# Splitting the first four convolutions of the up projection into an early and a late part

## The chip, the cores and the metric

The kernel runs on one core of a Trainium2 chip. The metric is the device time of one execution in microseconds (us). The core has five engines that run side by side and meet only through semaphores: TensorE (PE, matmuls into PSUM), VectorE (DVE), ScalarE (ACT), GpSimd (POOL) and SyncE (SP), which here only issues transfers. PSUM, the memory that TensorE writes, has eight banks of 128 x 512 float32 values.

## The reference

One layer of a hybrid block on x of 256 rows and 2048 columns: three kinds of attention, a gate, an output projection, then a feed-forward part. Only the feed-forward part matters here:

```python
h2 = rms_norm(x, g_ffn[l])
u = causal_depthwise_conv(h2 @ w_up[l], conv_w[l], conv_b[l])   # 3 taps along the rows
u_gate, u_val = jnp.split(u, 2, axis=-1)                        # 5632 columns each
x = x + (jax.nn.silu(u_gate) * u_val) @ w_down[l]
```

All arithmetic is float32.

## The kernel before, in words

A float32 product is made of cheaper ones: each weight tile `raw` is split into a high half `hi` (a cast on ACT, L141) and a low half `lo` (raw minus hi, a subtraction on DVE, L142), and TensorE multiplies both. `piece` (L135 to L146) is one such step: SP loads 128 x 1024 values, ACT casts, DVE subtracts. There are four buffers each for raw, hi and lo, so ACT can cast a piece only when TensorE has finished with the piece four before it, and SP can load a piece only when the low half of the piece four before it is made.

The up stage goes over `w_up` in groups of four column tiles of 128 (the loop over `f0`), for the gate half (s = 0) and the value half (s = 1) of each. A group is eight pieces (k = 0, 2, ..., 14); each piece is eight pairs of matmuls: L1148 (hi, 512 wide) and L1149 (lo, 256 wide). A group fills four PSUM banks, and the next group the other four. Its names are `u_0`, `hi_u_0_6`, `lo_u_1_8` and so on: the first number is s, the second k. The third group is called `u_0` again (f0 = 4, s = 0). Here "first group" is f0 = 0, s = 0, "second" is f0 = 0, s = 1, "third" is f0 = 4, s = 0.

After a group four convolutions follow, one per bank (`conv`, L1109 to L1132). Each empties its bank (ACT copies one half to `cr`, L1114; DVE adds the other, L1116), multiplies by `rbc` on DVE (L1117, into a padded tile `u`), applies tap 2 and the bias on ACT (L1120), the two other taps on DVE (L1121, L1122), and then either a Silu on ACT (s = 0, L1124) or, for s = 1, the product with the gate half and a split into halves for the next stage (L1128, L175, L176).

`rbc` is the reciprocal root of the mean square of each row of x, laid along the free dimension and repeated on all partitions. It isn't there when the up stage starts: the first group of matmuls runs on rows that aren't normalised yet, and the sums of squares come in meanwhile. When they are done (L551 to L534 in the trace), POOL stores 256 numbers to DRAM (L1044, `rstd_row`) and loads them back to all partitions (L1045, `rbc`).

The order: convolutions are generators that `later` queues; `tick`, called after each piece, advances at most two of them (WINDOW) by one step. Instructions are then put by a scheduler into one fixed order per engine, which each engine follows strictly; `in_order` (`keep_in_program_order`) pins an instruction to its place in the program among the pinned ones. Beside all this `weight_sums` adds up parts of the later stage's weights (`pre_d`, DVE L267 to L269), with loads on SP's queue (L258).

Of the kernel before, what the change touches and what calls it, by code (L numbers as in the profile page):

```python
# [9 lines left out]
F32 = mybir.dt.float32  # L10
F32R = mybir.dt.float32r
AF = mybir.ActivationFunctionType
ALU = mybir.AluOpType
AX = mybir.AxisListType

P = 128
S = 256
# [24 lines left out]
def hybrid_block(  # L42
# [25 lines left out]
    nc = tc.nc  # L68
# [12 lines left out]
    def bank(name):  # L81
        return pp.tile([P, 512], F32, tag="bank", name=name)
# [14 lines left out]
    def later(gen):  # L97
        waiting.append(gen)
# [3 lines left out]
    def tick(beside=True):  # L102
        if beside:
            for g in background:
                next(g, None)
        while waiting and len(active) < WINDOW:
            active.append([waiting.popleft(), 0])
        for a in list(active):
            if a[1] > 0:
                a[1] -= 1  # L110
                continue
            try:
                a[1] = next(a[0]) or 0
            except StopIteration:
                active.remove(a)
# [19 lines left out]
    def piece(src, a, n, name):  # L135
        raw = wp.tile([P, PIECE], F32, tag="raw", name=f"raw_{name}")
        hi = wp.tile([P, PIECE], F32R, tag="hi", bufs=SBUFS, name=f"hi_{name}")
        lo = wp.tile([P, PIECE], F32R, tag="lo", bufs=SBUFS, name=f"lo_{name}")
        m = a * n
        pin(nc.sync.dma_start(raw[:, :m].rearrange("p (a n) -> p a n", a=a), src))  # L140
        pin(nc.scalar.copy(hi[:, :m], raw[:, :m]))  # L141
        pin(nc.vector.tensor_tensor(lo[:, :m], raw[:, :m], hi[:, :m].bitcast(F32), ALU.subtract))  # L142
        return (
            hi[:, :m].rearrange("p (a n) -> p a n", a=a),
            lo[:, :m].rearrange("p (a n) -> p a n", a=a),
        )  # L146
# [9 lines left out]
    def product(x_of, w, nk, n0, n, name):  # L156

        ps = [bank(f"{name}_{t}") for t in range(NT)]
        wv = w.rearrange("(k p) n -> p k n", p=P)
        for k in range(0, nk, 2):  # L160
            a = min(2, nk - k)
            wh, wl = piece(wv[:, k : k + a, n0 : n0 + n], a, n, f"{name}_{k}")
            order = [(j, t) for j in range(a) for t in range(NT)]
            if k + a == nk:
                order.sort(key=lambda jt: jt[1])
            for j, t in order:
                xk = x_of(k + j)
                xs_ = xk[:, t * P : (t + 1) * P], xk[:, S + t * P : S + (t + 1) * P]
                three(ps[t][:, :n], *xs_, (wh[:, j], wl[:, j]), k + j == 0, k + j == nk - 1)
            tick()  # L170
        return ps

    def split_to(dst, src):

        nc.scalar.copy(dst[..., :S], src)  # L175
        nc.vector.tensor_tensor(dst[..., S:], src, dst[..., :S].bitcast(F32), ALU.subtract)  # L176
# [53 lines left out]
    in_order = tc.keep_in_program_order  # L230
# [343 lines left out]
    def plain_heads(ps, rs, name):  # L574
        y = rows_of(block(f"y_{name}"))
        for t in range(NT):
            nc.scalar.activation(y[:, t], ps[t], AF.Copy, scale=rs[:, t : t + 1])
        return y

    def norm_heads(ps, rs, name):  # L580

        y = plain_heads(ps, rs, name)
        ss = sm.tile([P, NT * 4], F32, tag="hss", name=f"hss_{name}")
        for t in range(NT):
            sq = junk(f"sq_{name}_{t}")
            nc.scalar.activation(sq, y[:, t], AF.Square)
            nc.vector.tensor_reduce(
                ss[:, t * 4 : (t + 1) * 4], sq.rearrange("p (h d) -> p h d", h=4), AX.X, ALU.add
            )
        r = sm.tile([P, NT * 4], F32, tag="hr", name=f"hr_{name}")  # L590
        rsqrt_mean(r, ss, NT * 4, HD, name)
        for t in range(NT):
            yt = y[:, t].rearrange("p (h d) -> p h d", h=4)
            nc.vector.tensor_tensor(
                yt, yt, r[:, t * 4 : (t + 1) * 4].unsqueeze(2).to_broadcast([P, 4, HD]), ALU.mult
            )
        return y
# [105 lines left out]
    y = norm_heads(kv[0], rstd_m, "mk")  # L703
# [26 lines left out]
    ps = proj(C_MQ, MEM_W, "mq")  # L730
# [5 lines left out]
    y = norm_heads(ps, rstd, "mq")  # L736
# [30 lines left out]
    for c in range(3):  # L767
        ps = proj(c * 512, 512, f"f{c}")
        qk[c] = heads_of(block(f"qk_fox{c}"))
        y = norm_heads(ps, rstd, f"f{c}")  # L770
# [5 lines left out]
    ps = proj(1536, 512, "f3")  # L776
# [3 lines left out]
    ps = proj(2048, 262, "f4")  # L780
# [74 lines left out]
    for c in range(3):  # L855
        ps = proj(C_SB + c * 512, 512, f"s{c}")
        qs[c] = heads_of(block(f"qk_sb{c}"))
        y = plain_heads(ps, rstd, f"s{c}")
# [49 lines left out]
    ps = proj(C_SB + 1536, 512, "s3")  # L908
# [4 lines left out]
    ps = proj(C_SB + 2048, 256, "s4")  # L913
# [39 lines left out]
    for m in range(2):  # L953
        gate = []
        for b, plan in enumerate(g_plans[m]):
# [40 lines left out]
            if not plan:  # L996
                biases()
                for n in range(2):
                    ps = proj(c0 + n * 512, 512, f"g{n}_{b}")
# [12 lines left out]
        for n in range(2):  # L1012
            acc = gate[branches[0][3]][n]
            for i, (w, k0, nk, b) in enumerate(branches):
                ps = product(lambda k: oT[:, k0 + k], w[0], nk, (2 * m + n) * 512, 512, f"b{2 * m + n}_{b}")
# [16 lines left out]
    rbc = cst.tile([P, S], F32, name="rbc")  # L1032
# [56 lines left out]
    def a_pair(p):  # L1089
        if p < FA // 2:  # L1090
            return aT[:, 2 * p : 2 * p + 2]
        if p not in ends:
            ends[p] = ff.tile([P, 2, 2 * S], F32R, tag=f"end{p - FA // 2}", bufs=1, name=f"end_{p}")
        return ends[p]

    uv = ctx.enter_context(ExitStack())
    cp = uv.enter_context(tc.tile_pool(name="cp", bufs=2))
    upv = w_up[0].rearrange("(k p) n -> p k n", p=P)
    pads = []

    def padded():
        for i in range(2):
            u = cp.tile([P, S + 2], F32, bufs=1, name=f"u_{i}")
            nc.vector.memset(u[:, 0:2], 0.0)
            pads.append(u)

    ys = {}

    def conv(ps, f, s):  # L1109
        if not pads:  # L1110
            padded()
        ct = s * FT + f
        cr = cp.tile([P, S], F32, tag="cr", bufs=2, name=f"cr_{f}_{s}")
        nc.scalar.copy(cr, ps[:, S:])  # L1114
        u = pads[f % 2]
        nc.vector.tensor_tensor(cr, cr, ps[:, :S], ALU.add)  # L1116
        nc.vector.tensor_tensor(u[:, 2:], cr, rbc, ALU.mult)  # L1117
        y = cp.tile([P, S], F32, tag="y", bufs=6, name=f"y_{f}_{s}")
        tap = lambda j: taps[:, j, ct : ct + 1]
        nc.scalar.activation(y, u[:, 2:], AF.Identity, scale=tap(2), bias=tap(3))  # L1120
        nc.vector.scalar_tensor_tensor(y, u[:, 1 : S + 1], tap(1), y, ALU.mult, ALU.add)  # L1121
        nc.vector.scalar_tensor_tensor(y, u[:, 0:S], tap(0), y, ALU.mult, ALU.add)  # L1122
        if s == 0:
            nc.scalar.activation(y, y, AF.Silu)  # L1124
            ys[f] = y
        else:
            g = ys.pop(f)
            nc.vector.tensor_tensor(g, g, y, ALU.mult)  # L1128
            split_to(a_pair(f // 2)[:, f % 2], g)
        return  # L1130
        yield

    for f0 in range(0, FT, 4):
        if f0 == FA:
            assert not halves
            for g in background:
                deque(g, 0)
            background.clear()
        for s in range(2):
            ps = [bank(f"u{f0 + i}_{s}") for i in range(4)]  # L1140
            c0 = s * D_FF + f0 * P
            for k in range(0, KT, 2):
                hi, lo = piece(upv[:, k : k + 2, c0 : c0 + 512], 2, 512, f"u{f0}_{s}_{k}")
                for j in range(2):
                    first, last = k + j == 0, k + j == KT - 1
                    for i in range(4):
                        c = slice(i * P, (i + 1) * P)
                        nc.tensor.matmul(ps[i], lhsT=hi[:, j, c], rhs=hT(k + j), start=first, stop=False)  # L1148
                        nc.tensor.matmul(  # L1149
                            ps[i][:, :S], lhsT=lo[:, j, c], rhs=hT(k + j)[:, :S], start=False, stop=last  # L1150
                        )
                tick()
            for i in range(4):
                later(conv(ps[i], f0 + i, s))

# [89 lines left out]
```

## Time and profile before

| | us |
|---|---|
| three runs: median (lowest to highest) | 1480.77 (1472.53 to 1480.96) |
| the profiled execution | 1473.09 |
| its span, first to last instruction | 1471.4 |
| PE busy | 1462.6 (99%) |
| DVE busy | 1192.1 (81%) |
| ACT busy | 838.9 (57%) |
| mean granted TensorE clock | 0.998 |

"Busy" of PE means that some matmul was in flight; a matmul that runs at a lower clock counts as busy for its longer time. An engine's line in a timeline gives the start, the duration, the line of the kernel, what is written and read, and in brackets how long the engine stood idle before it and what ended that. "SPq" and POOL lines of transfers are the issuing alone; "to landing" is the time until the data has arrived.

### The profile page before, as it was taken

What the parts mean: (1) busy time and instruction counts of PE and PEld (TensorE: products, weight loads), DVE (VectorE), ACT (ScalarE), POOL (GpSimd) and SP (SyncE); (2) the same over time, 40 slices, a digit from 0 to 9 for tenths busy, and PEclk for the clock granted to TensorE, in tenths of its full rate; (3) what the DMA queues carried; (4) which work ended last, traced back from release to release, by engine and by line L of the source; (5) the groups of instructions that cost most, each with busy time, mean ns of one, the idle gap of its engine ahead of it and who ended that gap; (6) DMA issues with size and microseconds to landing.
All of it is one profiled execution on the core that took longest, in us unless ns stands there. A gap on an engine that the chain in (4) does not pass through costs nothing.

```text
span 1471.4 us, 20662 instructions
## 1 busy us (share of the span) xinstructions
PE 1462.6 (99%) x7335; PEld 1236.9 (84%) x7335; DVE 1192.1 (81%) x1816; ACT 838.9 (57%) x1194; POOL 21.7 (1%) x48
## 2 busy tenths in 40 slices
PE   9999999999999999999999999999999999999998
PEld 7888888888888888888887888888888888888887
DVE  5777676777588899997877888888899877997877
ACT  6755454464364455546665556556556565674664
POOL 0000000021000000000000000000000000000000
PEclk9999999999999999999999999999999999999999
DMA  9686787687868576878777998888888866798795
GB/s 310 200 275 192 218 285 215 185 273 217 248 197 277 165 230 201 277 254 274 244 191 239 298 288 283 278 285 286 286 287 285 266 191 200 243 322 273 249 339 218
DMA packets 205606, 369.55 MB, mean 251 GB/s; under 512 B 13578, under 2 KB 82078, under 8 KB 205246
## 3 DMA queue, kind: packets, MB, share of 16 engines
q1 hardware_dynamic: 204094, 365.99, 78.0%
q10 hardware_dynamic: 1328, 2.11, 0.4%
q8 instruction: 57, 0.93, 0.2%
q14 instruction: 47, 0.39, 0.1%
q0 software_dynamic: 80, 0.13, 0.0%
HBM read 335.67 MB, written 32.51 MB: 250 GB/s over the span
## 4 chain that ended last, share of the span: by engine, by line
PE 97%; issue 1%; ACT 1%; DVE 1%; DMA 0%; POOL 0%; POOLq 0%; DVEq 0%
PE u L1148 21%; PE u L1149 11%; PE xd L286 4%; PE xd L288 4%; PE xd L287 4%; PE xg L288 3%; PE xg L287 3%; PE xg L286 3%; PE f L288 2%; PE f L287 2%; PE f L286 2%; PE s L286 2%; PE s L288 2%; PE s L287 2%; PE g L286 2%; PE g L288 2%
## 5 line engine op out<-in xcount | busy, mean ns | idle before, releaser
L1148 PE MATMUL u<-hT,hi_u 128*128 128x512 f32 x1232 | 430.8, 395 | 0.0
L1149 PE MATMUL u<-hT,lo_u 128*128 128x256 f32 x1232 | 342.7, 278 | 3.4 <-DVE lo_u L142 3.4
L1148 PEld LDWEIGHTS u<-hT,hi_u 128*128 128x128 f32 x1232 | 232.3, 189 | 54.0
L142 DVE TENSOR_TENSOR lo_u<-raw_u,hi_u 128x1024 fp32r<-128x1024 f32 x176 | 214.7, 1221 | 61.7 <-ACT hi_u L141 60.7
L141 ACT CAST hi_u<-raw_u 128x1024 fp32r<-128x1024 f32 x176 | 184.6, 1050 | 136.4 <-PE u L1148 120.5
L1149 PEld LDWEIGHTS u<-hT,lo_u 128*128 128x128 f32 x1232 | 232.6, 189 | 3.8 <-DVE lo_u L142 3.8
L281 DVE TENSOR_TENSOR lo_d<-raw_d,hi_d 128x1024 fp32r<-128x1024 f32 x88 | 106.6, 1221 | 20.4 <-ACT hi_d L280 17.6
L280 ACT CAST hi_d<-raw_d 128x1024 fp32r<-128x1024 f32 x88 | 91.9, 1053 | 47.8 <-PE xd L287 22.5
L280 ACT CAST hi_g<-raw_g 128x1024 fp32r<-128x1024 f32 (+1 forms) x64 | 61.7, 972 | 37.9 <-PE xg L287 12.1
L281 DVE TENSOR_TENSOR lo_g<-raw_g,hi_g 128x1024 fp32r<-128x1024 f32 (+1 forms) x64 | 70.8, 1117 | 4.1 <-ACT hi_g L280 4.1
L141 ACT CAST hi_f<-raw_f 128x1024 fp32r<-128x1024 f32 (+1 forms) x40 | 38.6, 967 | 52.1 <-PE f L287 47.3
L142 DVE TENSOR_TENSOR lo_f<-raw_f,hi_f 128x1024 fp32r<-128x1024 f32 (+1 forms) x40 | 44.6, 1118 | 27.9 <-ACT hi_f L141 26.1
L288 PE MATMUL xd<-lo_d,aT 128*128 128x512 f32 x170 | 66.2, 389 | 0.0
L287 PE MATMUL xd<-hi_d,aT 128*128 128x512 f32 x170 | 66.2, 389 | 0.0
L286 PE MATMUL xd<-hi_d,aT 128*128 128x512 f32 x170 | 66.1, 389 | 0.0
L142 DVE TENSOR_TENSOR lo_s<-raw_s,hi_s 128x1024 fp32r<-128x1024 f32 (+1 forms) x40 | 44.7, 1117 | 25.0 <-ACT hi_s L141 24.7
L141 ACT CAST hi_s<-raw_s 128x1024 fp32r<-128x1024 f32 (+1 forms) x40 | 38.4, 961 | 43.9 <-PE s L287 27.0
L1120 ACT ACTIVATE y<-u,taps 128x256 f32<-128x256 f32 x88 | 49.2, 595 | 23.8 <-DVE u L1117 23.8
L1148 PE MATMUL u<-hT_rest,hi_u 128*128 128x512 f32 x176 | 62.1, 394 | 0.0
L142 DVE TENSOR_TENSOR lo_g<-raw_g,hi_g 128x1024 fp32r<-128x1024 f32 x32 | 39.3, 1232 | 22.7 <-ACT hi_g L141 22.4
L141 ACT CAST hi_b<-raw_b 128x1024 fp32r<-128x1024 f32 x32 | 33.5, 1051 | 40.8 <-PE b L287 15.0
L141 ACT CAST hi_g<-raw_g 128x1024 fp32r<-128x1024 f32 x32 | 33.5, 1051 | 37.3 <-PE g L287 35.4
(479 smaller groups left out, 3530.3 us busy)
## 6 DMA issues: line engine op xcount, KB each, us to landing
raw_u<-in_w_up_dram SPq DMA_DIRECT2D x176, 512.0 KB, 5.2
raw_g<-in_w_in_dram SPq DMA_DIRECT2D x96, 512.0 KB, 4.4
raw_d<-in_w_down_dram SPq DMA_DIRECT2D x66, 512.0 KB, 5.3
pre_d<-in_w_down_dram SPq DMA_DIRECT2D x88, 256.0 KB, 4.4
kept_d<-pre_d SPq DMA_DIRECT2D x44, 512.0 KB, 5.5
raw_f<-in_w_in_dram SPq DMA_DIRECT2D x32, 512.0 KB, 4.7
raw_s<-in_w_in_dram SPq DMA_DIRECT2D x32, 512.0 KB, 3.8
raw_o<-in_w_out_dram SPq DMA_DIRECT2D x25, 512.0 KB, 5.4
```

The lines of the kernel that those rows point to most:

```text
L141: pin(nc.scalar.copy(hi[:, :m], raw[:, :m]))
L142: pin(nc.vector.tensor_tensor(lo[:, :m], raw[:, :m], hi[:, :m].bitcast(F32), ALU.subtract))
L280: nc.scalar.copy(hi[:, :n], src)
L281: nc.vector.tensor_tensor(lo[:, :n], src, hi[:, :n].bitcast(F32), ALU.subtract)
L286: fix(nc.tensor.matmul(o, lhsT=ah, rhs=w[0], start=first, stop=False))
L287: fix(nc.tensor.matmul(o, lhsT=al, rhs=w[0], start=False, stop=False))
L288: fix(nc.tensor.matmul(o, lhsT=ah, rhs=w[1], start=False, stop=last))
L1120: nc.scalar.activation(y, u[:, 2:], AF.Identity, scale=tap(2), bias=tap(3))
L1148: nc.tensor.matmul(ps[i], lhsT=hi[:, j, c], rhs=hT(k + j), start=first, stop=False)
L1149: nc.tensor.matmul(ps[i][:, :S], lhsT=lo[:, j, c], rhs=hT(k + j)[:, :S], start=False, stop=last)
```

## The change: four convolutions in two parts

Only the four convolutions of the first group are changed. `conv` is cut into `out_of` (empties a bank) and `taken` (multiplies by rbc, taps, Silu). A new generator `first_convs` calls `out_of` for all four banks in its first two steps, into the tiles `y` instead of `cr`, then lets steps pass (`yield 3`) and calls `taken` for one convolution per step, its multiplication by `rbc` pinned. All other groups go through `conv`, which does what it did.

```diff
+    def out_of(ps, dst):
+        nc.scalar.copy(dst, ps[:, S:])
+        nc.vector.tensor_tensor(dst, dst, ps[:, :S], ALU.add)
+        return dst
+
+    def y_tile(f, s):
+        return cp.tile([P, S], F32, tag="y", bufs=6, name=f"y_{f}_{s}")
+
+    def taken(cr, y, f, s):
         ct = s * FT + f
-        cr = cp.tile([P, S], F32, tag="cr", bufs=2, name=f"cr_{f}_{s}")
-        nc.scalar.copy(cr, ps[:, S:])
         u = pads[f % 2]
-        nc.vector.tensor_tensor(cr, cr, ps[:, :S], ALU.add)
-        nc.vector.tensor_tensor(u[:, 2:], cr, rbc, ALU.mult)
-        y = cp.tile([P, S], F32, tag="y", bufs=6, name=f"y_{f}_{s}")
+        ins = nc.vector.tensor_tensor(u[:, 2:], cr, rbc, ALU.mult)
+        if y is not None:
+            in_order(ins)
+        y = y_tile(f, s) if y is None else y
...
+    def conv(ps, f, s):
+        taken(out_of(ps, cp.tile([P, S], F32, tag="cr", bufs=2, name=f"cr_{f}_{s}")), None, f, s)
...
+    def first_convs(ps):
+        kept = []
+        padded()
+        for f in range(4):
+            kept.append(out_of(ps[f], y_tile(f, 0)))
+            if f % 2:
+                yield
+        yield 3
+        for f in range(4):
+            taken(kept[f], kept[f], f, 0)
+            yield
...
+            if f0 + s == 0:
+                later(first_convs(ps))
+                continue
```

The order on PE, POOL and SP is the same as before. On ACT the rows of the same convolutions move along with DVE's. On DVE it differs in some 60 rows, at two places. The first is the start of the second group. Before, DVE's rows there are (numbers at the end of a name tell buffers apart):

```order
L142 TENSOR_TENSOR lo_u_1_4_7044<-raw_u_1_4_7042,hi_u_1_4_7043 128x1024
L1116 TENSOR_TENSOR cr_0_6984<-cr_0_6984,u_0_6715 128x256
L1116 TENSOR_TENSOR cr_0_6993<-cr_0_6993,u_0_6716 128x256
L1117 TENSOR_TENSOR u_6980<-cr_0_6984,rbc 128x256
L1117 TENSOR_TENSOR u_6982<-cr_0_6993,rbc 128x256
L142 TENSOR_TENSOR lo_u_1_6_7066<-raw_u_1_6_7064,hi_u_1_6_7065 128x1024
```

In the changed kernel, the rows behind the low half of k = 4:

```order
L1111 TENSOR_TENSOR y_0_6984<-y_0_6984,u_0_6715 128x256
L1111 TENSOR_TENSOR y_0_6987<-y_0_6987,u_0_6716 128x256
L1111 TENSOR_TENSOR y_0_7012<-y_0_7012,u_0_6717 128x256
L142 TENSOR_TENSOR lo_u_1_6_7042<-raw_u_1_6_7040,hi_u_1_6_7041 128x1024
L1111 TENSOR_TENSOR y_0_7015<-y_0_7015,u_0_6718 128x256
L142 TENSOR_TENSOR lo_u_1_8_7064<-raw_u_1_8_7062,hi_u_1_8_7063 128x1024
L142 TENSOR_TENSOR lo_u_1_10_7086<-raw_u_1_10_7084,hi_u_1_10_7085 128x1024
L142 TENSOR_TENSOR lo_u_1_12_7108<-raw_u_1_12_7106,hi_u_1_12_7107 128x1024
L267 TENSOR_TENSOR pre_d_4_1_7128<-pre_d_4_1_7128 128x512
L268 TENSOR_TENSOR pre_d_4_1_7128<-pre_d_4_1_7128 128x256
L269 TENSOR_TENSOR pre_d_4_1_7128<-pre_d_4_1_7128 128x256
L1120 TENSOR_TENSOR u_6980<-y_0_6984,rbc 128x256
```

The first row that reads `rbc` stood ahead of the low half of k = 6; it now stands behind that of k = 12 and the sums of `pre_d_4_1`.

The second place is the third group, on DVE as well. Before, when its piece k = 4 has been split, the convolutions of the second group begin and the low half of k = 6 follows four rows later:

```order
L142 TENSOR_TENSOR lo_u_0_4_7281<-raw_u_0_4_7279,hi_u_0_4_7280 128x1024
L1116 TENSOR_TENSOR cr_1_7213<-cr_1_7213,u_1_6954 128x256
L1116 TENSOR_TENSOR cr_1_7224<-cr_1_7224,u_1_6955 128x256
L1117 TENSOR_TENSOR u_6980<-cr_1_7213,rbc 128x256
L1117 TENSOR_TENSOR u_6982<-cr_1_7224,rbc 128x256
L142 TENSOR_TENSOR lo_u_0_6_7303<-raw_u_0_6_7301,hi_u_0_6_7302 128x1024
```

In the changed kernel the last taps of the first group's convolutions (`y_0`) stand among those of the second group (`y_1`). Between the low halves of k = 4 and k = 6 are thirteen rows; the first eight of them are:

```order
L142 TENSOR_TENSOR lo_u_0_4_7255<-raw_u_0_4_7253,hi_u_0_4_7254 128x1024
L1111 TENSOR_TENSOR cr_1_7204<-cr_1_7204,u_1_6954 128x256
L1126 TENSOR_SCALAR y_0_7015<-u_6982,taps,y_0_7015 128x256
L1120 TENSOR_TENSOR u_6980<-cr_1_7204,rbc 128x256
L1127 TENSOR_SCALAR y_0_7015<-u_6982,taps,y_0_7015 128x256
L1111 TENSOR_TENSOR cr_1_7242<-cr_1_7242,u_1_6955 128x256
L1126 TENSOR_SCALAR y_1_7208<-u_6980,taps,y_1_7208 128x256
L1120 TENSOR_TENSOR u_6982<-cr_1_7242,rbc 128x256
L1127 TENSOR_SCALAR y_1_7208<-u_6980,taps,y_1_7208 128x256
```

The low half of k = 6 moved from the fifth row behind that of k = 4 to the fourteenth; the low half of k = 8 comes nine rows behind that of k = 6 (before, twelve). From about k = 2 of the fourth group on the two orders are the same again.

More of the change, by code (lines that the diff above doesn't have):

```diff
@@ L1107, in hybrid_block @@
     ys = {}
-    def conv(ps, f, s):
-        if not pads:
-            padded()
+    def out_of(ps, dst):
[5 more added lines that the diff above has]
+    def taken(cr, y, f, s):
         ct = s * FT + f
-        cr = cp.tile([P, S], F32, tag="cr", bufs=2, name=f"cr_{f}_{s}")
-        nc.scalar.copy(cr, ps[:, S:])
         u = pads[f % 2]
-        nc.vector.tensor_tensor(cr, cr, ps[:, :S], ALU.add)
-        nc.vector.tensor_tensor(u[:, 2:], cr, rbc, ALU.mult)
-        y = cp.tile([P, S], F32, tag="y", bufs=6, name=f"y_{f}_{s}")
+        ins = nc.vector.tensor_tensor(u[:, 2:], cr, rbc, ALU.mult)
+        if y is not None:
+            in_order(ins)
+        y = y_tile(f, s) if y is None else y
         tap = lambda j: taps[:, j, ct : ct + 1]
```

## The prediction

> **What bounds the kernel now.** I read the page first, then TensorE's waits, then the timelines around the one wait that matters.
>
> ```profile
> span 1471.4 us, 20662 instructions
> PE 1462.6 (99%) x7335; PEld 1236.9 (84%) x7335; DVE 1192.1 (81%) x1816; ACT 838.9 (57%) x1194; POOL 21.7 (1%) x48
> ...
> PE 97%; issue 1%; ACT 1%; DVE 1%; DMA 0%; POOL 0%; POOLq 0%; DVEq 0%
> ```
>
> The chain that ends last is TensorE for 97% of the span. So only what makes TensorE idle, or slow, can be gained or lost. These are all waits of TensorE's matmuls in the whole execution:
>
> ```profile
> PE u L1149 <- DVE lo_u L142: 3.4, 1, 3.4
> PE spare L91 <- DVE qscale L487: 1.2, 1, 1.2
> PE r L895 <- DVE ls L891: 0.2, 1, 0.2
> ```
>
> One wait of 3.4 us is in the up stage. Its cause is in DVE's order, and in POOL's transfers:
>
> ```profile
> 768.97 1.23 DVE L142 TENSOR_TENSOR lo_u<-raw_u,hi_u 128x1024 fp32r<-128x1024 f32 x1 [1.55 <-ACT hi_u L141]
> 770.13 0.77 DVE L1116 TENSOR_TENSOR cr<-cr,u 128x256 f32<-128x256 f32 x2
> 780.77 0.76 DVE L1117 TENSOR_TENSOR u<-cr,rbc 128x256 f32<-128x256 f32 x2 [9.87 <-DMA rbc<-rstd_row]
> 781.45 1.22 DVE L142 TENSOR_TENSOR lo_u<-raw_u,hi_u 128x1024 fp32r<-128x1024 f32 x1
> 770.66 1.05 ACT L141 CAST hi_u<-raw_u 128x1024 fp32r<-128x1024 f32 x1 [0.20 <-PE u L1148]
> 764.48 0.86 POOL L1044 DMA_DIRECT2D rstd_row<-scales  x1 [395.59 <-DVE scales L534]
> 773.64 0.57 POOL L1045 DMA_DIRECT2D rbc<-rstd_row  x1 [8.29 <-DMA rstd_row<-scales]
> ```
>
> The high half of the second group's piece k = 6 is cast by 771.7 (770.66 + 1.05). Its low half is made at 781.45, because two multiplications by `rbc` stand ahead of it and DVE stands idle for 9.87 us until `rbc` has landed. TensorE has pieces in hand for some 6 of these 10 us, and no more:
>
> ```profile
> 775.77 0.40 PE L1148 MATMUL u<-hT,hi_u 128*128 128x512 f32 x1
> 778.89 0.39 PE L1148 MATMUL u<-hT,hi_u 128*128 128x512 f32 x1
> 782.72 0.58 PE L1149 MATMUL u<-hT,lo_u 128*128 128x256 f32 x1 [3.44 <-DVE lo_u L142]
> 783.53 0.41 PE L1149 MATMUL u<-hT,lo_u 128*128 128x256 f32 x1
> 788.53 0.27 PE L1149 MATMUL u<-hT,lo_u 128*128 128x256 f32 x1
> 784.00:786.00 2.00, 2.00 (x7) 1.71 (x7) 2.00 (x6) 1.99 (x4) 0.00 (x0) 0.50 0.73 244
> ```
>
> The columns of the last row are the stretch, its length, busy time of PE, PEld, DVE, ACT, POOL, the granted clock, the DMA share and GB/s. Behind the wait the granted clock is 0.50, until the matmul at 788.53.
>
> **What the wait costs.** From 775.77 to 778.89 are nine pairs of matmuls, so a pair takes 0.347 us and a piece (eight pairs) 2.77. The L1149 that belongs to the L1148 at 778.89 would start about 0.23 later, at 779.12; it starts at 782.72, 3.60 late. From 782.72 to 788.53 again nine pairs are started; they take 5.81 instead of 3.12, which loses 2.69 more. The place costs **6.29 us**, and the half clock is over a third of it.
>
> Here the Trainium skill can be weighed. "TensorE: Matmul & The Clock Gate", section "What's actually happening", says that an idle window of about 3.4 us halves the clock and a busy one of as much restores it. The idle time (3.44) agrees; the half clock lasted some 5.5 us here, not 3.4. With the page's figure the slow part would cost 1.7 and the place 5.3; the trace's own 6.29 is used. The page also lets a shorter wait go without the clock penalty, which no row here can show, since the trace has only this one long wait inside the stages.
>
> **The change, part by part.** The number of instructions is the same: as many ACT copies, DVE additions, multiplications and taps. What moves:
>
> (1) The four evacuations come together. Two more ACT copies and two more DVE additions (0.33 us each, by the rows below) come ahead of or around the low half of k = 6. That delays it by under 1 us, against a deadline 6 us away. Cost nothing; the cover is the pieces that TensorE holds.
>
> (2) The multiplications by `rbc` go behind the low half of k = 12. The removed wait: 6.29 us, if nothing else is late. What is late next are the loads, because the 16 DMA engines carry little just then:
>
> ```profile
> 767.00:775.00 8.00, 8.00 (x48) 7.00 (x47) 2.36 (x4) 2.83 (x4) 0.57 (x1) 1.00 0.76 51
> 775.00:781.00 6.00, 4.28 (x25) 3.49 (x23) 0.23 (x1) 0.00 (x0) 0.00 (x0) 1.00 0.86 302
> 765.82 0.37 SPq L140 DMA_DIRECT2D raw_u<-in_w_up_dram  x1
> raw_u<-in_w_up_dram SPq DMA_DIRECT2D x1, 512.0 KB, 11.2
> 770.22 0.37 SPq L140 DMA_DIRECT2D raw_u<-in_w_up_dram  x1
> raw_u<-in_w_up_dram SPq DMA_DIRECT2D x1, 512.0 KB, 10.4
> 770.63 1.10 SPq L258 DMA_DIRECT2D pre_d<-in_w_down_dram  x1
> pre_d<-in_w_down_dram SPq DMA_DIRECT2D x1, 256.0 KB, 10.7
> rbc<-rstd_row POOLq DMA_DIRECT2D x1, 128.0 KB, 7.0
> ```
>
> For eight microseconds they move 51 GB/s, then 302. The load issued at 765.82 is piece k = 8 (SP's order from there: k = 8, 10, 12, then `pre_d`). It lands 11.2 us later, at 777.0; cast (1.05) and subtraction (1.22) end at 779.3. TensorE needs this low half at 779.12 + 2.77 = 781.9. So it is in time by 2.6 us: cost nothing. Piece k = 12 lands at 770.22 + 10.4 = 780.6, is cast by 781.7 and split by 782.9, against a deadline of 787.4. `pre_d` lands by 770.63 + 10.7 = 781.3, `rbc` at 773.64 + 7.0 = 780.6. So neither the sums of `pre_d` nor `rbc` is waited for: **the pinned multiplication finds its data**, about 3.8 us old.
>
> (3) All taps of the first group come later, and DVE has them beside the second group's convolutions. The rows for DVE's pace when it is never out of work:
>
> ```profile
> 802.15 0.88 DVE L1122 SCALAR_TENSOR_TENSOR y<-u,taps,y 128x256 f32<-128x256 f32 x2
> 802.95 0.75 DVE L1128 TENSOR_TENSOR y<-y,y 128x256 f32<-128x256 f32 x2
> 803.62 0.41 DVE L1116 TENSOR_TENSOR cr<-cr,u 128x256 f32<-128x256 f32 x1
> 807.55 1.22 DVE L142 TENSOR_TENSOR lo_u<-raw_u,hi_u 128x1024 fp32r<-128x1024 f32 x1
> 808.69 0.42 DVE L1128 TENSOR_TENSOR y<-y,y 128x256 f32<-128x256 f32 x1
> 791.12 0.68 DVE L267 TENSOR_TENSOR pre_d<-pre_d 128x512 f32<-128x512 f32 x1
> 792.64 2.35 DVE L142 TENSOR_TENSOR lo_u<-raw_u,hi_u 128x1024 fp32r<-128x1024 f32 x2
> 790.00:813.00 23.00, 23.00 (x135) 20.12 (x134) 22.76 (x41) 14.07 (x21) 0.00 (x0) 1.00 0.93 309
> ```
>
> From start to start a tap takes 0.40, a 256-wide two-tile operation 0.335, a low half 1.14, the three sums of `pre_d` 1.52. After k = 12 (782.9) come the sums, so the first multiplication starts at 784.4. From it to the end of the low half of the third group's k = 8, the changed order on DVE has 40 rows: 17 two-tile operations (5.7), 14 taps (5.5), 6 low halves (6.8) and one set of sums (1.3, mixed with other rows): 19.4 us, so that low half ends at 803.8. Its deadline: the third group would start its first L1149 at 779.12 + 5 x 2.77 = 793.0, and k = 8 is four pieces on, 804.1. That is the tightest place, **0.3 us of slack**. The low half of k = 6, nine rows earlier, has about 1.5. The sum holds only if DVE never waits for ACT in these 19 us. Before, in the 23 us behind the wait, DVE did keep busy 22.76, with no wait of TensorE; but there the taps came in twos, and now each convolution goes ACT to DVE and back by itself. Bounds for what is left: nothing, or, if each of the eight convolutions in that stretch makes DVE wait as long as one tap (0.40), 3.2 - 0.3 = 2.9 us. I take 0.5, nearer to the first, since the row of DVE's dense stretch is the nearest one.
>
> The PSUM banks of the first group are free far earlier, which is worth nothing: no row of TensorE's waits names a bank.
>
> **Sum.** 6.29 - 0.5 = 5.8 us less. The profiled execution took 1473.09, so 1467.3; of its 1.7 us outside the span nothing changes. The three runs' median, 1480.77, is 7.7 above the profiled execution, the lowest run (1472.53) beside it. The profile doesn't show where the other two runs spent 8 us more; if the changed kernel is measured at that level, the same step gives 1475.0. One per cent, about what a measurement of this kernel can tell from no change, is 14.8 us: more than twice the whole step.
>
> **Rivals.** (a) DVE's jam in the third group is as bad as its upper bound: 2.9 us of waiting is left, below the 3.44 us behind which the clock fell. Gain 3.4, time 1469.7. For it: the slack of 0.3. Against it: DVE's 22.76 of 23 busy without harm.
>
> (b) `rbc` comes later, because loads that were held up before now start earlier and share the DMA engines with it. SP's next load, k = 14, was issued at 782.70 and can now go out by 774.8, beside the transfer of `rbc` (issued 773.64):
>
> ```profile
> 782.70 0.37 SPq L140 DMA_DIRECT2D raw_u<-in_w_up_dram  x1
> ```
>
> 512 KB at 302 GB/s are 1.7 us, so `rbc` would land at 782.4, still ahead of 784.4: cost nothing. Only one load can be that early, since the next waits for the low half of k = 8 at 779.3. The Trainium skill's "DMA: Bandwidth & Descriptors", section "Issuing engines are not separate DMA queues", speaks for the sharing: all issuers' transfers run on the same 16 engines and interleave. Beyond that, every microsecond past 784.4 holds all of DVE's queue behind the pinned multiplication, and goes straight into the tight place.
>
> (c) **Slower than before:** the same mechanism with a late `rbc`. The point from which it decides is 788.3: landed 3.9 us behind its turn at 784.4, `rbc` would make the third group's k = 8 wait 3.6 with the clock halved behind it, all that was removed. At 793, some 12 us later, TensorE waits 8.3 and loses 2.7 to the clock, 11.0 in all against the 6.29 removed: 1477.8. The two transfers would have to take 28 us instead of 16 (764.48 to 780.6).
>
> (d) The change doesn't do what it says, in part: the wait goes, but the clock falls at this time for a reason other than the wait. Gain 3.6, time 1469.5. Against it: the clock is 1.00 up to the wait.
>
> (e) The 8 us by which the runs differ arise in this wait too (a later `rbc`), and the change takes them as well: 1480.77 becomes 1467 or a little less, which is a gain just around 1%.
>
> **How the numbers follow.** Forecast (0 to 1.5 us of wait left, at either level of the runs) 0.62; (a) 0.14; (b) with a cost 0.03; (c) 0.04; (d) 0.04; (e) 0.13. The time is the forecast's from the profiled execution, 1467. The range goes from 1464 (the whole 6.29 off the lowest run, 1466.2, and some scatter) to 1477 (the forecast at the median's level, 1475.0, and (a)'s 2.4 us on top, nearly). Faster by over 1%: most of (e), 0.11; slower by over 1%: 0.03, from the far end of (c); within 1%: 0.86.
>
> **What would show it.** In the changed profile DVE's multiplications by `rbc` (L1120 there) have no idle time ahead of them; TensorE's longest wait is under 2 us and, if there is one, stands at a low half of the third group, k = 6 to 10; the granted clock stays 1.00 around 780 to 790; the second group takes 22.2 us. A wait at the second group's k = 8 would show the loads as the next bound. The prediction is wrong if the clock still falls in this stretch, or if DVE waits for ACT for more than 3 us between 784 and 804.

## The result

The changed kernel takes 1468.85 us (median of 22 runs, 1466.9 to 1477.5), the kernel before, measured beside it, 1480.64 (22 runs, 1472.17 to 1482.69). The ratio of the two, after to before, is 0.995 with a 95% interval of 0.9932 to 0.9967: about 7.4 us less, half a per cent, faster by more than its measurement is uncertain and less than the one per cent of the prediction. The two medians lie further apart, 11.8 us, only because they fall into different groups of runs. The profiled execution of the changed kernel took 1476.86 us.

Both kernels' runs lie in two groups 8 us apart. Before: 6 runs near 1473.0 and 16 near 1481.0; after: 13 near 1467.9 and 9 near 1476.6 (medians of the groups). The profiled execution of before was one of the lower group, that of after is one of the upper, so the two spans can't be compared without knowing what the 8 us are. The traces tell it, below.

From the page of the changed kernel, and the list of all waits of TensorE's matmuls:

```profile
span 1475.1 us, 20662 instructions
PE 1469.3 (100%) x7335; PEld 1240.1 (84%) x7335; DVE 1193.8 (81%) x1816; ACT 839.8 (57%) x1194; POOL 21.8 (1%) x48
...
PE spare L91 <- DVE qscale L487: 1.2, 1, 1.2
PE u L1169 <- DVE lo_u L142: 0.5, 1, 0.5
PE r L895 <- DVE ls L891: 0.2, 1, 0.2
```

The wait of 3.4 us is gone and one of 0.5 is left in its stage. DVE's and ACT's timelines around the change, and TensorE's around the wait that is left (L1120 is now the multiplication by `rbc`, L1168 and L1169 are the matmuls with the high and the low half; the x1 or x3 at the end of a row counts the instructions that the row stands for):

```profile
783.40 1.23 DVE L142 TENSOR_TENSOR lo_u<-raw_u,hi_u 128x1024 fp32r<-128x1024 f32 x1 [0.81 <-ACT hi_u L141]
784.54 0.69 DVE L267 TENSOR_TENSOR pre_d<-pre_d 128x512 f32<-128x512 f32 x1
786.07 0.42 DVE L1120 TENSOR_TENSOR u<-y,rbc 128x256 f32<-128x256 f32 x1
804.41 1.22 DVE L142 TENSOR_TENSOR lo_u<-raw_u,hi_u 128x1024 fp32r<-128x1024 f32 x1
778.67 1.05 ACT L141 CAST hi_u<-raw_u 128x1024 fp32r<-128x1024 f32 x1 [5.76 <-DMA raw_u<-in_w_up_dram]
782.32 1.05 ACT L141 CAST hi_u<-raw_u 128x1024 fp32r<-128x1024 f32 x1 [0.98 <-DMA raw_u<-in_w_up_dram]
804.75 0.39 PE L1168 MATMUL u<-hT,hi_u 128*128 128x512 f32 x1
805.68 0.39 PE L1169 MATMUL u<-hT,lo_u 128*128 128x256 f32 x1 [0.55 <-DVE lo_u L142]
805.91 0.39 PE L1168 MATMUL u<-hT,hi_u 128*128 128x512 f32 x1
```

The multiplication at 786.07 has no idle time ahead of it: `rbc` and the sums' data were there. What is left is the wait for the low half of k = 8 of the third group, made at 804.41 to 805.63; the matmul that needs it starts at 805.68 instead of 804.98 (0.23 behind its L1168), 0.70 late. The next pair starts 1.16 behind the last one instead of 0.347, so the place costs 0.81 in all. The clock is granted in full all the while:

```profile
780.00:790.00 10.00, 10.00 (x59) 8.76 (x58) 8.74 (x13) 6.60 (x8) 0.00 (x0) 1.00 0.99 344
804.00:806.00 2.00, 1.45 (x9) 1.05 (x8) 2.00 (x5) 1.40 (x3) 0.00 (x0) 1.00 0.41 158
```

**The two groups of runs.** TensorE's first and last L1168 of two stretches of the changed kernel, before and behind its wait:

```profile
800.93 0.40 PE L1168 MATMUL u<-hT,hi_u 128*128 128x512 f32 x1
804.40 0.40 PE L1168 MATMUL u<-hT,hi_u 128*128 128x512 f32 x1
848.66 0.40 PE L1168 MATMUL u<-hT,hi_u 128*128 128x512 f32 x1
852.90 0.40 PE L1168 MATMUL u<-hT,hi_u 128*128 128x512 f32 x1
```

Eleven rows make ten pairs in 3.47 us, 0.347 us a pair; behind the wait thirteen rows make twelve pairs in 4.24, 0.353. The granted clock is 1.00 in both, and TensorE is never idle. The slower pace holds to the end of the up stage: 1248 pairs are left there (half a group and 19 groups of 64), at 6.7 ns more each 8.4 us. That is the distance between the groups of runs. In the profiled execution of before the pace is 0.347 behind the wait too. So there are two questions for the experiments: whether the step that was predicted is right at equal pace (1473.0 to 1467.9 is 5.1 us, 1481.0 to 1476.6 is 4.4; predicted 5.8), and whether it is the wait that decides the pace.

### The profile page after: what moved, and what is told of

Same layout as the page of the kernel before. It is cut to its first block, busy times and chain, and to the rows that moved or that the text cites. A ratio compares the mean times of both kernels' runs of the same rounds, so it can differ in the third digit from the quotient of the medians.

```text
span 1475.1 us, 20662 instructions
## 1 busy us (share of the span) xinstructions
PE 1469.3 (100%) x7335; PEld 1240.1 (84%) x7335; DVE 1193.8 (81%) x1816; ACT 839.8 (57%) x1194; POOL 21.8 (1%) x48
## 4 chain that ended last, share of the span: by engine, by line
PE 98%; DVE 1%; ACT 0%; issue 0%; POOL 0%; POOLq 0%; DVEq 0%
PE u L1168 22%; PE u L1169 11%; PE xd L288 4%; PE xd L286 4%; PE xd L287 4%; PE xg L287 3%; PE xg L286 3%; PE xg L288 3%; PE f L288 2%; PE f L287 2%; PE f L286 2%; PE s L286 2%; PE s L288 2%; PE s L287 2%; PE g L286 2%; PE g L288 2%
## 5 line engine op out<-in xcount | busy, mean ns | idle before, releaser
L1168 PE MATMUL u<-hT,hi_u 128*128 128x512 f32 x1232 | 435.6, 398 | 0.0
L1169 PE MATMUL u<-hT,lo_u 128*128 128x256 f32 x1232 | 345.6, 281 | 0.5 <-DVE lo_u L142 0.5
L1168 PEld LDWEIGHTS u<-hT,hi_u 128*128 128x128 f32 x1232 | 231.5, 188 | 57.3
L1169 PEld LDWEIGHTS u<-hT,lo_u 128*128 128x128 f32 x1232 | 232.6, 189 | 0.9 <-DVE lo_u L142 0.9
L1168 PE MATMUL u<-hT_rest,hi_u 128*128 128x512 f32 x176 | 63.1, 398 | 0.0
```

The source lines that it names most:

```text
L1169: nc.tensor.matmul(ps[i][:, :S], lhsT=lo[:, j, c], rhs=hT(k + j)[:, :S], start=False, stop=last)
```

## The experiments

Theory 1 is that of the prediction: the price is the wait for `rbc` with the half clock behind it, and the place of the multiplication in DVE's order decides. Theory 2 is new: after any wait in the up stage TensorE goes on at one of two paces.

**No rbc at all, and no wait left.** The first kernel has the order of before, but multiplies by something that is there:

```diff
+    rb_or_not = xres[:, 0, :S]
...
-        nc.vector.tensor_tensor(u[:, 2:], cr, rbc, ALU.mult)
+        nc.vector.tensor_tensor(u[:, 2:], cr, rb_or_not, ALU.mult)
```

> The kernel before, but every convolution multiplies by a slice of x's rows that has been there for long, instead of by rbc: the row normalisation is left out, the order is that of before, and nothing can wait for rbc. Theory 1 (the wait for rbc costs 3.6 us of idle time and 2.7 of half clock): TensorE has no wait in the up stage, the clock stays 1.00, and the time is 6.3 us less than before at the same pace of the matmuls, 1466.8. Theory 2, on the 8 us between single runs (1473 and 1481 before, 1468 and 1476 after): after any wait in the up stage TensorE goes on at one of two paces, 0.347 or 0.353 us a pair, until the stage ends. Without a wait it keeps 0.347, so all runs lie near 1467. Rival to theory 2: the pace is drawn by each execution, wait or not; then some runs lie near 1475.

The second is the changed kernel, with the second group's convolutions moved away from the tight place:

```diff
     def conv(ps, f, s):
+        if f < 4:
+            yield 1
         taken(out_of(ps, ...), None, f, s)
```

> The changed kernel, with the four convolutions of the second group begun one step later each, so that the low halves of the third group's k = 6 and 8 stand nine and twelve rows earlier on DVE. Theory 1: the wait at the third group's k = 8 (0.7 us late there) is gone and none takes its place; 0.7 us less than the changed kernel at the same pace, 1467. Theory 2: with no wait left, all runs lie near 1467 and none near 1476, so the median is some 13 us under that of before. Rival to theory 2: both levels remain, in about the shares of the changed kernel (9 of 22 runs upper). Rival to theory 1: a wait of 0.5 to 2 us comes at k = 10 to 14, where the work now lies.

(Counted in steps, the convolutions of the second kernel begin two later, not one as the expectation has it; the rows it names on DVE are right.) Measured: the first 1466.85 us (10 runs, 1466.3 to 1467.31), ratio to before 0.9945 (0.9925 to 0.9964); the second 1467.05 (10 runs, 1466.44 to 1469.47), ratio 0.9933 (0.9911 to 0.9955). The kernel before in the same series: 16 of 33 runs near 1472.6, 17 near 1481.1. All waits of TensorE, first kernel, then second:

```profile
PE spare L91 <- DVE qscale L487: 1.2, 1, 1.2
PE kv L153 <- DVE memT L184: 0.3, 1, 0.3
PE r L895 <- DVE ls L891: 0.2, 1, 0.2
```

```profile
PE spare L91 <- DVE qscale L487: 1.2, 1, 1.2
PE kv L152 <- ACT memT L181: 0.8, 1, 0.8
PE b L288 <- DVE lo_b L142: 0.3, 1, 0.3
PE kv L153 <- DVE memT L184: 0.2, 1, 0.2
```

The lists name no wait of the up stage (its tile is `u`; the others belong to other stages), and of twenty runs none is in an upper group. The first kernel isn't quite free of delays: one low half of the second group, that of k = 10, is ready at 784.94, and its matmul starts at 785.00, 0.22 late, which the list doesn't name and which costs some 0.3 us; the pace behind it is 0.347 all the same. Theory 1's price at equal pace is 1472.6 - 1466.85 = 5.8 us, against 6.29 from the one profiled execution. The wait that the change leaves costs 1467.9 - 1467.05 = 0.9, against 0.81 in its trace. Theory 2 holds in these runs: without a listed wait all stay at 0.347. The second kernel computes the whole of the reference, and its median is 13.1 us under that of before and 1.8 under that of the changed kernel: the best version here.

**The early emptying alone.** The pin is taken off, everything else of the change stays:

```diff
         ins = nc.vector.tensor_tensor(u[:, 2:], cr, rbc, ALU.mult)
-        if y is not None:
-            in_order(ins)
```

> The changed kernel without the pin on the multiplications by rbc: the four banks are emptied early as in the change, but the scheduler puts the first two multiplications ahead of the low half of k = 6 again. Theory 1 (place of the multiplication decides, the early emptying is worth nothing): the wait is back at k = 6, 3 to 4 us, with the clock at 0.50 behind it, and the time is that of before, 1473 or 1481. Rival (the early emptying gives a part): at least 2 us less than before.

Measured: ratio 0.9999 (0.997 to 1.0028); five runs near 1472.8, four from 1480.2 to 1483.3, and one of 7366 us, which nothing here explains and which the ratio leaves out. The wait is back:

```profile
PE u L1167 <- DVE lo_u L142: 3.3, 1, 3.3
```

So this wait hangs on the place of the multiplication, and emptying four banks at once is by itself worth nothing that can be measured. The granted clock is 0.50 behind the wait here too, but for half as long as in the profiled execution of before (the first row is of before, the second of this kernel):

```profile
781.60:788.30 6.70, 5.58 (x18) 4.81 (x19) 6.63 (x14) 6.46 (x12) 0.00 (x0) 0.50 0.36 86
783.90:787.20 3.30, 3.30 (x12) 2.73 (x11) 3.30 (x6) 3.29 (x7) 0.00 (x0) 0.50 0.70 173
```

**The emptying late as well.** Each of the four convolutions stays in one piece, and is held back by pins behind the low halves of k = 8 to 14 of the second group:

```diff
     def first_convs(ps):
-        kept = []
         padded()
-        for f in range(4):
-            kept.append(out_of(ps[f], y_tile(f, 0)))
-            if f % 2:
-                yield
         yield 3
         for f in range(4):
-            taken(kept[f], kept[f], f, 0)
+            y = y_tile(f, 0)
+            nc.scalar.copy(y, ps[f][:, S:])
+            in_order(nc.vector.tensor_tensor(y, y, ps[f][:, :S], ALU.add))
+            taken(y, y, f, 0)
             yield
```

The low halves of k = 8, 10 and 12 of the second group are pinned too (in `piece`, not shown), so that the convolutions stay behind them.

> The changed kernel with the emptying of the banks late too: each of the first four convolutions as a whole comes behind the low half of k = 8, 10 or 14 of the second group, so the banks stay full until then. Theory 1 (banks are not waited for, since the third group that needs them begins some 22 us after the first one ended): as the changed kernel within 1 us at the same pace. Rival: TensorE waits for a bank at the start of the third group, 1 us or more.

Measured: 1472.72 us (10 runs, 1470.85 to 1482.19), ratio 0.9991 (0.9964 to 1.0018). The expectation missed by some 4 us at equal pace (six runs from 1470.85 to 1472.9, with a median of 1472.3, against 1467.9). The rival's reason is not in the trace either, for no wait names a bank. All waits in the up stage are for low halves, at k = 12 of the second group and k = 6 of the third:

```profile
788.55 0.39 PE L1170 MATMUL u<-hT,lo_u 128*128 128x256 f32 x1 [0.33 <-DVE lo_u L142]
806.41 0.74 PE L1170 MATMUL u<-hT,lo_u 128*128 128x256 f32 x4 [2.79 <-DVE lo_u L142]
808.00:810.00 2.00, 2.00 (x8) 1.69 (x7) 2.00 (x4) 0.00 (x0) 0.00 (x0) 0.50 0.78 248
```

DVE's rows show a reason: with one convolution at a time, and the order pinned, DVE waits for ACT within the first two, and once for `rbc`.

```profile
781.65 0.42 DVE L1123 TENSOR_TENSOR u<-y,rbc 128x256 f32<-128x256 f32 x1 [0.70 <-DMA rbc<-rstd_row]
782.75 0.48 DVE L1129 SCALAR_TENSOR_TENSOR y<-u,taps,y 128x256 f32<-128x256 f32 x1 [0.67 <-ACT y L1128]
786.35 0.48 DVE L1129 SCALAR_TENSOR_TENSOR y<-u,taps,y 128x256 f32<-128x256 f32 x1 [0.67 <-ACT y L1128]
```

Such waits use up the slack of the third group, as rival (a) of the prediction had it for the change itself. The low half of k = 6 also stands sixteen rows behind that of k = 4 here, three more than in the changed kernel; the two were not tried apart. So a late multiplication by itself isn't enough: with each convolution in one piece, pinned behind those low halves, almost nothing is left of the gain. The 2.79 us were enough for the clock to fall. This trace also has the pace change twice, at its two waits. First and last L1169 (here the high half's matmul) of three stretches, ahead of the first wait, between the two, and behind the second:

```profile
783.66 0.39 PE L1169 MATMUL u<-hT,hi_u 128*128 128x512 f32 x1
786.78 0.40 PE L1169 MATMUL u<-hT,hi_u 128*128 128x512 f32 x1
796.89 0.40 PE L1169 MATMUL u<-hT,hi_u 128*128 128x512 f32 x1
802.55 0.40 PE L1169 MATMUL u<-hT,hi_u 128*128 128x512 f32 x1
848.77 0.40 PE L1169 MATMUL u<-hT,hi_u 128*128 128x512 f32 x1
852.93 0.40 PE L1169 MATMUL u<-hT,hi_u 128*128 128x512 f32 x1
```

They are 9, 16 and 12 pairs: 0.347, 0.354 and 0.347 us a pair. A wait can slow the pace and another can bring it back.

**A wait made elsewhere.** To the kernel without waits, a wait of chosen length is added far from all this, in the middle of the up stage:

```diff
                 for k in range(0, KT, 2):
+                    if (f0, s, k) == (20, 0, 12):
+                        held = junk("held")
+                        in_order(nc.vector.tensor_copy(held, lo[:, 0].bitcast(F32)))
+                        for _ in range(10):
+                            in_order(nc.vector.tensor_tensor(held, held, held, ALU.subtract))
                     hi, lo = piece(...)
```

There are 10, 12 or 16 such operations. The low halves of k = 10 and 12 of that group are pinned too (in `piece`, not shown), so that the extra operations stand between them.

> The kernel without any wait in the up stage (the one with the second group's convolutions begun a step later), with ten extra operations on DVE, each on the result of the one before, ahead of the low half of k = 12 in the eleventh of the 22 groups. They take some 0.72 us each, 7.7 with the copy ahead of them, against some 6 us that TensorE has in hand, so TensorE waits once, some 1.6 us. The clock stays 1.00 if a wait has to be near 3 us to lower it (0.5 us did not, 2.8 us did). Theory 2 (a wait makes TensorE go on at one of two paces, 0.347 or 0.353 us a pair): two levels, 1468.7 for the runs that keep 0.347, and 720 pairs x 6.7 ns = 4.8 us more, 1473.5, for the others. Rival (the pace was set by the early place, the change of the clock or the convolutions there): one level, 1468.7.

> The same with twelve operations: a wait of some 3.0 us. If the clock falls behind it for some 5 us as before, that adds 2.7: levels 1472.8 and, by theory 2, 1477.6. If it doesn't fall: 1470.1 and 1474.9.

> The same with sixteen operations: a wait of some 5.9 us, with the clock at 0.50 behind it for some 5 us: levels 1475.7 and, by theory 2, 1480.5.

The waits came out at 1.63 us, 3.09 and 5.99; with 10 operations a second one of 1.63, which wasn't expected, came at k = 6 of the next group. TensorE's matmul behind the first wait of each, with the clock of a stretch behind it, in the order 10, 12, 16 operations:

```profile
990.21 0.74 PE L1179 MATMUL u<-hT,lo_u 128*128 128x256 f32 x4 [1.63 <-DVE lo_u L142]
992.00:994.00 2.00, 2.00 (x14) 1.72 (x13) 2.00 (x4) 0.00 (x0) 0.00 (x0) 1.00 0.86 262
```

```profile
991.82 0.91 PE L1179 MATMUL u<-hT,lo_u 128*128 128x256 f32 x4 [3.09 <-DVE lo_u L142]
992.00:994.00 2.00, 2.00 (x9) 1.81 (x10) 2.00 (x4) 0.00 (x0) 0.00 (x0) 0.56 0.77 175
```

```profile
996.09 1.22 PE L1179 MATMUL u<-hT,lo_u 128*128 128x256 f32 x4 [5.99 <-DVE lo_u L142]
996.00:998.00 2.00, 1.91 (x7) 1.81 (x8) 2.00 (x4) 0.00 (x0) 0.00 (x0) 0.50 0.72 161
```

The runs: with 10 operations 1468.96, 1468.97, 1473.57 and 1474.98 (ratio 0.9931, 0.9912 to 0.9951); with 12, six runs from 1475.73 to 1477.35 (0.9969, 0.9951 to 0.9988); with 16, three from 1474.55 to 1476.01 and seven from 1479.15 to 1481.17 (0.9998, 0.9975 to 1.0021). Theory 2 said 1468.7 and 1473.5, 1472.8 and 1477.6, 1475.7 and 1480.5. Two groups came for 10 and 16, some 5.3 and 4.6 us apart against the 4.8 expected, about half of the 8.4 of a wait at the start of the stage, since only 720 pairs follow. With 12, all six runs are slow ones: they lie between the slow level without a fall of the clock (1474.9) and that with it (1477.6). The profile with 10 operations shows the pace change in the same execution (first and last row of 13, so twelve pairs, ahead of the waits and behind them):

```profile
948.79 0.40 PE L1178 MATMUL u<-hT,hi_u 128*128 128x512 f32 x1
952.95 0.40 PE L1178 MATMUL u<-hT,hi_u 128*128 128x512 f32 x1
1038.70 0.40 PE L1178 MATMUL u<-hT_rest,hi_u 128*128 128x512 f32 x1
1042.94 0.40 PE L1178 MATMUL u<-hT,hi_u 128*128 128x512 f32 x1
```

0.347, then 0.353. The rival, that the early place or its half clock sets the pace, is out: here neither is there. In each of the profiled runs with a wait the pace behind the last wait fits the group that the run fell into.

Not only a wait changes the pace, though. In all nine traces the up stage begins with sixteen pairs at the slow pace, until sixteen transposes (L195) are put between; behind them it is 0.347. Here are the second and the last of these pairs and the transposes, from the second kernel without a wait (14 pairs in 4.95 us, 0.354 a pair):

```profile
747.50 0.40 PE L1170 MATMUL u<-hT,hi_u 128*128 128x512 f32 x1
752.45 0.40 PE L1170 MATMUL u<-hT,hi_u 128*128 128x512 f32 x1
752.81 1.91 PE L195 MATMUL hT<-ident,xres_again 128*128 128x128 f32 x16
```

And in the kernels with extra operations the scheduler puts up to eight high halves' matmuls ahead of the low halves' at that place, and later four low ones in a row. With 16 operations the pace, once the clock is back at 1.00, is 0.347 until four low ones in a row at 1002.41, and 0.353 only from there on, without idle time; with 10 it is 0.347 for six pairs behind the second wait (1005.18 to 1007.26) before it is 0.353. So there the wait and the changed order of the matmuls were not tried apart. In the changed kernel and in that of before the order around the wait is even, and both groups of runs came.

## Why the prediction was right, and where it was off

- **The wait and its price.** Right, a little too high. 6.29 us were read from one execution; 33 runs of before against the kernel that needs no `rbc` give 5.8 at equal pace. The half clock isn't of one length: it was granted at 0.50 for 6.83 us in that execution (781.54 to 788.37, of which 1.2 lie in the wait) and for 3.41 in the kernel without the pin. Of the 16 lower ones among the 33 runs, four have a mean clock of 1.000 (1471.38 to 1472.03 us), so at most 1.5 us at half clock (an estimate from the rounding), and three have 0.997 (1473.58 to 1474.21). So the price differs by some 2 us from run to run.
- **What is late next.** Right: the loads came first (ACT waited 5.76 us for piece k = 8, DVE's low half was in time), and neither `rbc` nor the sums' data was waited for. Rivals (b) and (c) did not come up, since `rbc` was there at 786.07.
- **The tight place.** Named right, the third group's k = 8, and 0.5 us was taken for it; the trace has 0.55 us of idle time, 0.70 of delay and 0.81 in all, and the runs say 0.9. With the 5.8 above that makes a step of 4.9 where 5.8 was forecast. Of its working the long term was right (its four terms add up to 19.3, since 14 taps of 0.40 are 5.6 and not 5.5): the 19.4 us from the first multiplication to the end of that low half took 19.6 (786.07 to 805.63), and DVE did not wait for ACT. The chain started late, though. Piece k = 12 was expected in at 780.6, 781.5 on the changed kernel's trace, whose up stage begins 0.9 us later; it was cast at 782.32, 0.8 behind that, and the slack of 0.3 was used up.
- **The loads in that place.** Loads that could now go out earlier may have shared the DMA engines with piece k = 12, as rival (b) had it for `rbc`. The traces fit that: the load of k = 12 took 10.4 and 10.6 us in the two kernels where that of k = 14 goes out late (before, and without the pin), and 10.8 to 11.9 in the seven where it goes out early. That is one trace each, and it was not tried.
- **Rival (a)**, 2.9 us of waiting, was priced without a fall of the clock. It didn't come, but its price was too low: the kernel with the late emptying waited 2.79 us, and its clock fell.
- **The banks.** Right: the kernel without the pin empties them as early and gains nothing, and with them full for longer no wait names a bank.
- **The 8 us between runs.** Rival (e) said that they arise in this wait, which was right, and gave a later `rbc` as the reason, which was wrong: it is the pace at which TensorE goes on behind the wait. It also had the change take the 8 us away, which only the kernel begun later still does. The change takes the wait from 3.4 us to 0.5 but doesn't remove it, so the paces are still drawn, with 9 of 22 runs slow instead of 16. The mean gain of 7.4 us is therefore made of some 4.8 us of the step (5.1 and 4.4 in the two groups) and some 2.6 from that shift: 7 of 22 runs by 8.2 us. That the shares differ because of the shorter wait is not shown; the kernel before had 16 of 22 runs slow in one series, 17 of 33 in the next and 9 of 15 in the third, so part of the shift may be chance.
- **The time.** 1467 was the lower group's time and that group's median is 1467.9. The overall median, 1468.85, lies just above it because 13 of 22 runs fell there. The prediction had no reason for that share: with three more runs in the upper group the median would have been some 1475, so that it came so near is in part luck.
- **The clock rule of the Trainium skill**, "TensorE: Matmul & The Clock Gate", section "What's actually happening", has an idle window of about 3.4 us that lowers the clock. It agrees only roughly with what fell and what didn't: waits of 0.55 and 1.63 us left the clock at 1.00, and those of 2.79 and 3.09, shorter than the page's figure, lowered it in their traces as 5.99 did. Not every run behaves so: with 12 operations one of six has a mean clock of 1.000. The half clock lasted 3.41 us behind the waits of 2.79, 3.09 and 3.30, and 6.83, twice that, behind 3.44 and 5.99. So the prediction's "some 5.5 us, not 3.4" was two such lengths, the first of them begun inside the wait.

## What to carry to other kernels

Read a wait of TensorE with what follows it: here 3.4 us of idle time cost some 6, because of the clock, and in many runs 8 more, because of a slower pace to the end of the stage. A wait of half a microsecond can cost as much in that second way, so the last small wait in a long uniform stage is worth removing; beginning four convolutions a little later did it. When runs of one kernel fall into two groups, compare the spacing of equal instructions ahead of and behind each wait before looking for a lost or gained instruction.

## What the runs showed of the hardware

TensorE's stream of alternating 512 and 256 wide matmuls, each with its own weights, runs at 0.347 or at 0.353 us a pair, both at a granted clock of 1.00 and without idle time. The pace held for hundreds of pairs and changed where the even stream was broken: at listed waits, in either direction, with and without a fall of the clock, and also without a wait, at transposes put between and where four low halves' matmuls stood in a row. In one trace it changed six pairs behind a wait, with nothing in the rows to show why. None of 20 runs of the two kernels without a listed wait in the stage was slow; of each kernel one run has a trace. What distinguishes the two paces inside TensorE stays open. The rows show only that the slow one repeats every three pairs, in steps of 0.35, 0.35 and 0.36 us.
